# Summing the seven products of a Strassen–Winograd pair in the accumulator banks, with the partial sums copied by ScalarE

## The chip, the cores and the metric

The kernel runs on one core of a Trainium2 chip. The metric is the device time of one execution in microseconds (us); lower is better. Engines are called PE (TensorE), DVE (VectorE), ACT (ScalarE), POOL (GpSimd) and SP (SyncE, here a queue that issues transfers).

## The reference

One layer of an encoder with two gated branches, run on two batches: a long one of 1024 rows and a short one of 512, with shared weights. Cut to what matters here:

```python
h = rms_norm(x, pre_w)
cols = jnp.einsum('bsd,dc->bsc', h, w_in)          # one wide projection
m_qk, m_v, m_o, m_z, m_i, m_f, a_qkv, a_z, gate = jnp.split(cols, ...)
y_m = mlstm_mixer(m_qk, m_v, m_o, m_i, m_f, ...) * silu(m_z)    # branch A, chunks of 128 rows
y_a = dilated_attention(a_qkv, rel_table) * silu(a_z)           # branch B
merged = g[:, :, 0] * (y_m @ w_pm) + g[:, :, 1] * (y_a @ w_pa)  # g = sigmoid(gate)
out = merged @ w_out
return x + rms_norm(out, post_w)
```

Everything is float32. `m_i` and `m_f` are the gates of branch A; their scans (a cumulative sum, a running maximum, exponentials) are the "lanes" below. The change is in the projection `h @ w_in` of the long batch alone.

## The kernel before

**The projection of the long batch.** `h` (1024 rows) and the weights are cut into 2 x 2 blocks, and each block product is made with seven half-size products instead of eight, in Winograd's form: `B11, T2, B21, T3, T1, T4, B22` name the seven combinations of blocks of `h`, which are made once and kept. Each product is float32 by three passes: both operands are split into a rounded high part and a rest (`vhi`, `vlo`; `phla`, `phlb` hold both parts), and `mm3` (L193 to L195) issues high x high, high x rest, rest x high into one bank of the accumulator (PSUM, eight banks, tiles named `d`). With m1 to m7 the seven products, the four output blocks need m1+m2, m1+m6+m7+m5, m1+m6+m7+m4 and m1+m6+m5+m3.

**Value groups** (`value_group`, before 246 us): four groups of columns (values and the gates of branch A), seven products each; a product is 48 matmuls of 128x322 into four banks, 12 to a bank. Group 0 has a path of its own. In groups 1 to 3 the order is B11, B21, T2, T3, T1, T4, B22; ACT copies the four banks of m1 (L555), DVE does the other 28 additions (L564 to L602). `out` splits each finished block into `vz` (ACT L458, DVE L459) and stores it; the buffers `vz`, `vzm` and `co` are few (3, 2, 3), so an ACT copy into `vz` waits until the store of an earlier one has landed. Weights are split ahead by `split` (ACT `vhi` L426, DVE `vlo` L427).

**Pairs** (`unit_pair`, 246 to 975 us): 38 pairs of 128-column units, seven products each, a product is 12 matmuls of 128x512 into one bank. In the order B11, T2, B21, T3, T1, T4, B22; ACT copies m1 (L651) and DVE makes seven additions (L654 to L665). The weights of the next pair are prepared beside it (POOL sums L628 to L646; ACT L609 and DVE L610 split them). What follows a pair on ACT and DVE depends on its kind: 12 "att" pairs, 8 "conv" pairs (`conv_unit`: for each of two halves ACT L676, DVE L678 twice, ACT L679, DVE L680), 8 "zo", 2 "az", 8 gates.

**Lanes** (`lanes`, L837 on) is a generator in four steps, run between the products of value groups 1 and 2. Step 1 transposes the gates on PE (L855), reads the result on ACT (L857, L858), and runs a chain over ACT and DVE (L860 to L879) that ends in `l_tt`; step 2 transposes `l_u` and `l_tt` on PE (L883, L884); step 3 transposes `l_mrow` (L904); step 4 transposes what a second chain made of it (L926, L927). The position of the steps is set by

```python
for g in range(1, 3):
    for j, _ in enumerate(values[g]):
        if j % 3 == 0:
            next(lanes, None)
```

where `j` counts the products of a group (in group 1 the first product has been issued ahead of the loop, so `j = 0` stands behind its second).

Each engine runs its instructions in the order in which they were issued; a scheduler places the copies, splits and additions of ACT and DVE among each other, and PE goes through the products in the order of the code. The stage after 975 us (branches, output projections; `dense`) is not touched.

Of the kernel before, what the change touches and what calls it, by code (L numbers as in the profile page):

```python
# [22 lines left out]
F32 = mybir.dt.float32  # L23
F32R = mybir.dt.float32r
AF = mybir.ActivationFunctionType
# [4 lines left out]
P = 128  # L30
D = 1024
KT = D // P
BLK = 512
# [12 lines left out]
VW = 322  # L46
# [25 lines left out]
class Tokens:  # L72


    def __init__(self, dram, S, x, y, name):
        self.S, self.x, self.y, self.n, self.nblk, self.name = S, x, y, S // P, S // BLK, name
        t = lambda shape, what, dt=F32: dram.tile(shape, dt, name=f"{what}_{name}")
        self.qk = t([16, P, S], "qk")
        self.vs = t([2, S, D], "vs")
        self.G = t([8, P, S], "G")  # L80
        self.aqk = t([2, 24, P, S], "aqk")
        self.av = t([S, 1536], "av")
        self.az = t([4, P, S], "az")
# [20 lines left out]
        return self.bufs[i][dt]  # L104


class Unit:


# [67 lines left out]
class Net:  # L177
# [9 lines left out]
        kw = {} if space is None else {"space": space}  # L187
        return stack.enter_context(self.tc.tile_pool(name=name, bufs=bufs, side=side, reuse_waits="tile", **kw))

    def mm3(self, out, lhs, rhs, start, stop):  # L190
        nc = self.nc
        (lh, ll), (rh, rl) = lhs, rhs
        nc.tensor.matmul(out, lh, rh, start=start, stop=False)  # L193
        nc.tensor.matmul(out, lh, rl, start=False, stop=False)  # L194
        nc.tensor.matmul(out, ll, rh, start=False, stop=stop)  # L195

# [206 lines left out]
    def value_group(self, g, T, H, sb, us, co, ps, late=None, begin=None, u3=None, more=None, turn=None):  # L403
# [17 lines left out]
        def split(x, at=None, parts=1):  # L421
            hi, lo = at or place()
            with self.tc.high_priority():
                for i in range(parts):
                    c = slice(i * N // parts, (i + 1) * N // parts)
                    ends = (nc.scalar.activation(hi[:, c], x[:, c], AF.Copy),  # L426
                            nc.vector.tensor_sub(lo[:, c], x[:, c], hi[:, c].bitcast(F32)))  # L427
# [3 lines left out]
        def product(m, w, turns=(), outer=False):  # L431

            banks = [ps.tile([P, BLK], F32, name="d") for _ in range(4)]
            turns = iter(turns)
            if outer:
                next(turns)
            for i in range(4):
                for j in range(4):
                    t, k = (j, i) if outer else (i, j)
                    ts = slice(t * P, (t + 1) * P)  # L440
                    self.mm3(banks[t][:, :VW], (H[0][m][:, k, ts], H[1][m][:, k, ts]), (w[0][:, k], w[1][:, k]),
                             k == 0, k == 3)
                next(turns, None)
            return banks

# [24 lines left out]
        if g == 0:  # L470
# [77 lines left out]
                add(u3[t], u3[t], m6[t][:, :VW])  # L548
            yield
            co = co()  # L550
        else:
            self.sums(wa, wb, s)
            m1 = product(B11, split(wa[:, 0], first))
            for t in range(4):
                nc.scalar.activation(u2[t], m1[t][:, :VW], AF.Copy)  # L555
            w12 = split(wa[:, 1])
            s2 = split(s[:, 1])
            nc.vector.tensor_sub(s[:, 1], wa[:, 1], s[:, 1])
            yield
            m2 = product(B21, w12)  # L560
            co = co()
            for t in range(4):
                c = tile_("co", 3)
                add(c, u2[t], m2[t][:, :VW])  # L564
                out(t, 0, 0, c)
            yield
            m6 = product(T2, s2)
            for t in range(4):
                add(u2[t], u2[t], m6[t][:, :VW])
            yield  # L570
            m7 = product(T3, split(wb[:, 0]))
            u3 = []
            for t in range(4):
                u3.append(tile_("u3", 4))
                add(u3[t], u2[t], m7[t][:, :VW])
            yield
        if g == 0:
            with self.tc.issue_after(low[2]):
                s1 = split(s[:, 0])
        else:  # L580
            s1 = split(s[:, 0])
        m5 = product(T1, s1)
        if g == 0:
            for t, c in enumerate(held):
                out(t, 0, 0, c)
        for t in range(4):
            add(u2[t], u2[t], m5[t][:, :VW])
            c = tile_("co", 3)
            add(c, u3[t], m5[t][:, :VW])
            out(t, 1, 1, c)  # L590
        yield
        if late is not None:
            store = lambda *x: late.append(x)
        m4 = product(T4, split(wb[:, 1]))
        for t in range(4):
            add(u3[t], u3[t], m4[t][:, :VW])  # L596
            out(t, 0, 1, u3[t])
        yield
        m3 = product(B22, split(s[:, 1]))
        yield  # L600
        for t in range(4):
            add(u2[t], u2[t], m3[t][:, :VW])  # L602
            out(t, 1, 0, u2[t])

    def pair_split(self, x, hl):
        n = x.shape[1]
# [7 lines left out]
    def pair_weights(self, ua, ub, sb):  # L614


        ws = []
        us = [sb.tile([P, BLK], F32, name=f"pu{i}", bufs=4 - i) for i in (2, 3)]
# [10 lines left out]
        self.nc.gpsimd.tensor_sub(s[:, 1], s[:, 0], ws[0][:, 0])  # L629
        s12 = self.pair_split(s, at[1])  # L630
        self.nc.gpsimd.tensor_sub(ws[1][:, 0], ws[0][:, 0], ws[1][:, 0])
        return (*ws, a1, s12, s, bs, us), last

    def unit_pair(self, weights, H, sb, cp, ps):

        nc = self.nc
        wa, wb, (a11, a12), (s1, s2), s, places, (u2, u3) = weights
        split = self.pair_split

        def product(m, w):  # L640
            p = ps.tile([P, BLK], F32, name="d")
            for k in range(4):
                self.mm3(p, (w[0][:, k], w[1][:, k]), (H[0][m][:, k], H[1][m][:, k]), k == 0, k == 3)
            return p

        nc.gpsimd.tensor_sub(s[:, 1], wa[:, 1], s[:, 1])  # L646
        s3, a22 = split(wb, places[0])
        c = [cp.tile([P, 2 + 2 * BLK], F32, name="c") for _ in range(2)]
        q = [[c[j][:, 1 + b * BLK:1 + (b + 1) * BLK] for b in range(2)] for j in range(2)]
        m1 = product(B11, a11)  # L650
        nc.scalar.activation(u2, m1, AF.Copy)  # L651
        m6 = product(T2, s2)
        m2 = product(B21, a12)
        nc.vector.tensor_add(q[0][0], u2, m2)  # L654
        nc.vector.tensor_add(u2, u2, m6)
        m7 = product(T3, s3)
        nc.vector.tensor_add(u3, u2, m7)
        m5 = product(T1, s1)
        nc.vector.tensor_add(q[1][1], u3, m5)
        nc.vector.tensor_add(u2, u2, m5)  # L660
        m4 = product(T4, a22)
        nc.vector.tensor_add(q[1][0], u3, m4)
        s4, = split(s[:, 1:2], places[1])
        m3 = product(B22, s4)
        nc.vector.tensor_add(q[0][1], u2, m3)  # L665
        return c


# [1164 lines left out]
def body(tc, a):  # L1833
# [3 lines left out]
    with ExitStack() as st:  # L1837
# [12 lines left out]
        with ExitStack() as s1:  # L1850
# [4 lines left out]
            with ExitStack() as sv:  # L1855
# [45 lines left out]
                for _ in values[0]:  # L1901
                    pass
                s3.close()
                more, turn = N.pool(sv, "more", 1, "left"), itertools.cycle(range(5))
                values += [N.value_group(g, A, H, vw, us, co, ps, late if g == 3 else None, more=more, turn=turn)
                           for g in range(1, 4)]
                next(values[1])
                with ExitStack() as s4:
                    lanes = N.lanes(A, N.pool(s4, "lane", 1, "right"), lambda: ps.tile([P, BLK], F32, name="d"))
                    for g in range(1, 3):  # L1910
                        for j, _ in enumerate(values[g]):
                            if j % 3 == 0:
                                with tc.issue_after(N.splits[0].ins), tc.issue_after(N.splits[1].ins):
                                    next(lanes, None)
                    for _ in lanes:
                        pass
                    N.bias_tables(N.pool(s4, "tab", 1, "right"), ps, dram)
# [199 lines left out]
```

## Time and profile before

| | us |
|---|---|
| median of 3 runs | 2289.6 (2284.14 to 2295.39) |
| profiled execution, time | 2292.12 |
| profiled execution, span from first to last instruction | 2290.3 |
| PE busy in the span | 2258.5 (99%) |
| DVE busy | 1465.7 (64%) |
| ACT busy | 1102.2 (48%) |
| POOL busy | 628.6 (27%) |
| granted clock of PE, mean | 0.997 |

The profile is of one execution. A row of the timeline begins with the start in us from the first instruction and the length in us (of all the instructions counted at its end); behind it stand the engine, the line, what is written and read, and in brackets how long the engine had been idle and what ended that. A row of the table by windows has the busy time of each engine in a stretch with its number of instructions; matmuls overlap, so a busy PE there need not be PE at its peak, but a PE that waits is seen.

### The profile page before, as it was taken

How to read it: one execution, taken by the hardware profiler on the slowest of the kernel's cores; microseconds unless marked ns; L12 is line 12 of the kernel's file. 1: busy time of each engine (PE TensorE's matmuls, PEld its weight loads, DVE VectorE, ACT ScalarE, POOL GpSimd, SP SyncE). 2: the span in 40 equal slices, each digit the busy share in tenths (PEclk: the TensorE clock that was granted, in tenths of full speed). 3: DMA queues.
4: the chain of work that ended last, by engine and by line, in shares of the span. 5: the costliest groups of instructions: out<-in, count | busy, mean ns of one | idle time of the engine just before them, and what ended most of it. 6: DMA issues, size and time to landing. Idle time of an engine off the chain costs nothing. (4 is left out here: it accounts for less than half of the span.)

```text
span 2290.3 us, 36121 instructions
## 1 busy us (share of the span) xinstructions
PE 2258.5 (99%) x12628; PEld 1975.3 (86%) x12628; DVE 1465.7 (64%) x2851; ACT 1102.2 (48%) x2255; POOL 628.6 (27%) x824
## 2 busy tenths in 40 slices
PE   9999999999999999999999999999999999999998
PEld 8999888888878888879999889988888888888887
DVE  7765577688875564466777756674487744555563
ACT  6332243444443343366667656776544444544422
POOL 2000333333332232136556510001032221421311
PEclk9999999999999999999999999999999999999999
DMA  3552455543222243285674679987687878787673
GB/s 126 161 134 71 173 204 194 195 167 113 101 102 83 83 147 110 91 315 154 219 226 138 199 195 243 249 227 214 181 254 242 254 217 241 201 256 210 216 259 113
DMA packets 251903, 416.71 MB, mean 182 GB/s; under 512 B 24993, under 2 KB 150049, under 8 KB 251722
## 3 DMA queue, kind: packets, MB, share of 16 engines
q1 hardware_dynamic: 248120, 401.82, 56.9%
q10 hardware_dynamic: 3602, 12.59, 1.4%
q8 instruction: 100, 1.64, 0.3%
q14 instruction: 81, 0.66, 0.1%
HBM read 294.34 MB, written 128.37 MB: 185 GB/s over the span
## 5 line engine op out<-in xcount | busy, mean ns | idle before, releaser
L193 PE MATMUL dense<-H,wh 128*128 128x512 f32 x672 | 277.5, 413 | 2.3 <-DVE sw L714 1.9
L195 PE MATMUL dense<-H,wl 128*128 128x512 f32 x672 | 263.8, 393 | 0.0
L194 PE MATMUL dense<-H,wh 128*128 128x512 f32 x672 | 263.0, 391 | 0.0
L195 PE MATMUL d<-Hh,phla 128*128 128x512 f32 x608 | 237.0, 390 | 2.2 <-DVE phla L610 2.2
L193 PE MATMUL d<-Hh,phla 128*128 128x512 f32 x608 | 236.6, 389 | 0.0
L194 PE MATMUL d<-Hl,phla 128*128 128x512 f32 x608 | 236.6, 389 | 0.0
L250 DVE TENSOR_TENSOR wl<-wraw,wh 128x1024 fp32r<-128x1024 f32 (+1 forms) x130 | 163.9, 1262 | 106.7 <-ACT wh L249 105.4
L1475 DVE CUSTOM_DVE_ANT_0 ls<-lg,bias 128x256 f32<-128x256 f32 (+1 forms) x288 | 93.7, 361 | 158.9 <-PE lg L1463 53.9
L249 ACT ACTIVATE wh<-wraw 128x1024 fp32r<-128x1024 f32 (+1 forms) x130 | 137.0, 1054 | 97.1 <-PE dense L194 50.0
L628 POOL TENSOR_TENSOR psum_w<-pw_raw 128x512 f32<-128x512 f32 x38 | 61.4, 1617 | 443.4 <-DVE u L596 216.0
L1479 ACT ACTIVATE ls<-ls,nm 128x256 f32<-128x256 f32 (+1 forms) x288 | 130.0, 453 | 102.9 <-DVE nm L1477 87.8
L195 PE MATMUL d<-Hh,phlb 128*128 128x512 f32 x456 | 177.4, 389 | 0.0
L193 PE MATMUL d<-Hh,phlb 128*128 128x512 f32 x456 | 177.4, 389 | 0.0
L194 PE MATMUL d<-Hl,phlb 128*128 128x512 f32 x456 | 177.4, 389 | 0.0
L195 PEld LDWEIGHTS dense<-H,wl 128*128 128x128 f32 x672 | 126.2, 188 | 28.7
L193 PEld LDWEIGHTS dense<-H,wh 128*128 128x128 f32 x672 | 126.6, 188 | 20.4 <-issue 2.3
L194 PEld LDWEIGHTS dense<-H,wh 128*128 128x128 f32 x672 | 127.0, 189 | 17.5
L194 PE MATMUL d<-vlo,Hh 128*128 128x322 f32 x448 | 139.9, 312 | 1.9 <-DVE vlo L427 1.9
L193 PE MATMUL d<-vhi,Hh 128*128 128x322 f32 x448 | 141.0, 315 | 0.3
L195 PE MATMUL d<-vhi,Hl 128*128 128x322 f32 x448 | 140.3, 313 | 0.4 <-DVE Hl L354 0.2
L195 PEld LDWEIGHTS d<-Hh,phla 128*128 128x128 f32 x608 | 114.1, 188 | 27.3 <-DVE phla L610 3.7
L194 PEld LDWEIGHTS d<-Hl,phla 128*128 128x128 f32 x608 | 114.1, 188 | 23.7
(573 smaller groups left out, 6064.2 us busy)
## 6 DMA issues: line engine op xcount, KB each, us to landing
pw_raw<-w_in SPq DMA_DIRECT2D x76, 512.0 KB
wraw<-w_in SPq DMA_DIRECT2D x76, 512.0 KB
aqk_a<-pwk SPq DMA_DIRECT2D x48, 512.0 KB
aqk_b<-sw SPq DMA_DIRECT2D x48, 256.0 KB
wraw<-w_pm SPq DMA_DIRECT2D x24, 512.0 KB
wraw<-w_out SPq DMA_DIRECT2D x24, 512.0 KB
wraw<-w_v SPq DMA_DIRECT2D x18, 512.0 KB
erep<-erow SPq DMA_DIRECT2D x16, 512.0 KB
```

The costliest lines, as they stand in the source:

```text
L193: nc.tensor.matmul(out, lh, rh, start=start, stop=False)
L194: nc.tensor.matmul(out, lh, rl, start=False, stop=False)
L195: nc.tensor.matmul(out, ll, rh, start=False, stop=stop)
L249: self.splits = (nc.scalar.activation(hi[:, :n], raw[:, :n], AF.Copy), nc.vector.tensor_sub(lo[:, :n], raw[:, :n], hi[:, :n].bitcast(F32)))
L250: nc.vector.tensor_sub(lo[:, :n], raw[:, :n], hi[:, :n].bitcast(F32)))
L628: self.nc.gpsimd.tensor_add(s[:, 0], ws[1][:, 0], ws[1][:, 1])
L1475: nc.vector.tensor_tensor_reduce(out=ls[:, hh], in0=ts["lg"][hh], in1=bt[:, hh], scale=1.0, scalar=NEG, op0=OP.add, op1=OP.max, accum_out= ...
L1479: nc.scalar.activation(ls[:, hh], ls[:, hh], AF.Exp, bias=nm[:, hh:hh + 1], accum_out=ot[:, 128 + hh:129 + hh])
```

## The change

The products are reordered and partial sums are built in the banks. A new class `Banks` hands out the eight banks by hand: `hold` takes one, `done` gives it back. With `onto`, a product goes on adding in a bank that already holds a sum. In a pair the order becomes B11, B21, T2, T1, T3, B22, T4:

```diff
-        m1 = product(B11, a11)
-        nc.scalar.activation(u2, m1, AF.Copy)
-        m6 = product(T2, s2)
-        m2 = product(B21, a12)
-        nc.vector.tensor_add(q[0][0], u2, m2)
-        nc.vector.tensor_add(u2, u2, m6)
-        m7 = product(T3, s3)
-        nc.vector.tensor_add(u3, u2, m7)
-        m5 = product(T1, s1)
-        nc.vector.tensor_add(q[1][1], u3, m5)
-        nc.vector.tensor_add(u2, u2, m5)
-        m4 = product(T4, a22)
-        nc.vector.tensor_add(q[1][0], u3, m4)
-        s4, = split(s[:, 1:2], places[1])
-        m3 = product(B22, s4)
-        nc.vector.tensor_add(q[0][1], u2, m3)
+        sum_ = product(B11, a11)
+        nc.scalar.activation(e1, sum_, AF.Copy)
+        m2 = product(B21, a12)
+        nc.vector.tensor_add(q[0][0], e1, m2)
+        ps.done([m2])
+        product(T2, s2, sum_)
+        nc.scalar.activation(e6, sum_, AF.Copy)
+        m5 = product(T1, s1)
+        nc.scalar.activation(e5, m5, AF.Copy)
+        product(T3, s3, sum_)
+        nc.vector.tensor_add(q[1][1], e5, sum_)
+        s4, = split(s[:, 1:2], places[1])
+        product(B22, s4, m5)
+        nc.vector.tensor_add(q[0][1], e6, m5)
+        ps.done([m5])
+        product(T4, a22, sum_)
+        nc.scalar.activation(q[1][0], sum_, AF.Copy)
+        ps.done([sum_])
```

So a pair has four copies on ACT and three additions on DVE, where it had one and seven. A product that adds onto a bank has to wait until the copy or addition that reads the bank's earlier sum is done: T2 for the copy `e1`, T3 for `e6`, B22 for `e5`, T4 for the addition into `q[1][1]`. The value groups 1 to 3 get the same order and sums, bank by bank (12 additions and 16 copies a group, where there were 28 and 4); group 0 keeps its own. The lanes' steps move too:

```diff
-                            if j % 3 == 0:
+                            if j in ((0, 1, 5), (0, 2, 6))[g - 1]:
```

On PE, step 1 of the lanes stays where it was, in the middle of value group 1. Step 2 stood 144 matmuls (three products) behind it, ahead of the product T4 (`Hh_617`):

```order
L193 MATMUL d<-vhi,Hh_100 128x322
L194 MATMUL d<-vlo,Hh_100 128x322
L195 MATMUL d<-vhi,Hl_107 128x322
L883 MATMUL d<-ident,l_u_1151 1x64
L884 MATMUL d<-ident,l_tt 1x64
L193 MATMUL d<-vhi,Hh_617 128x322
```

It stands 48 matmuls (one product, T2, `Hh_97`) behind it in the changed kernel, ahead of T1 (`Hh_100`):

```order
L211 MATMUL d<-vhi,Hh_97 128x322
L212 MATMUL d<-vlo,Hh_97 128x322
L213 MATMUL d<-vhi,Hl_104 128x322
L918 MATMUL d<-ident,l_u_1151 1x64
L919 MATMUL d<-ident,l_tt 1x64
L211 MATMUL d<-vhi,Hh_100 128x322
```

Two products that stood ahead of the two transposes now stand behind them. Likewise step 3 is now 194 matmuls behind step 2, and step 4 one product (48 matmuls) behind step 3.

On ACT, the chain of the lanes' step 1 ran like this in the kernel before (`l_e`, `l_l` are the lanes' tiles, `vzm` and `vhi` belong to the value group):

```order
L458 ACTIVATE vzm<-co 128x322
L860 ACTIVATE l_e<-l_lf 64x128
L861 ACTIVATE l_e<-l_e 64x128
L863 ACT_TABLE_LOAD
L863 ACTIVATE l_l<-l_u_1151 64x128
L865 ACT_TABLE_LOAD
L865 ACTIVATE l_e<-l_l 64x128
L426 ACTIVATE vhi<-vsum 128x1288
```

In the changed kernel the copies of T2's banks (`u2b<-d`) stand in it:

```order
L476 ACTIVATE vzm<-co 128x322
L592 ACTIVATE u2b<-d 128x322
L895 ACTIVATE l_e<-l_lf 64x128
L592 ACTIVATE u2b<-d 128x322
L896 ACTIVATE l_e<-l_e 64x128
L898 ACT_TABLE_LOAD
L898 ACTIVATE l_l<-l_u_1151 64x128
L592 ACTIVATE u2b<-d 128x322
L900 ACT_TABLE_LOAD
L900 ACTIVATE l_e<-l_l 64x128
L444 ACTIVATE vhi<-vb 128x1288
```

Three copies have come in, and the split `vhi` of the next weights still stands behind the chain.

In a conv pair, ACT ran this from one split of weights to the next in the kernel before:

```order
L609 ACTIVATE phlb<-pw_raw 128x1024
L609 ACTIVATE phlb<-psum_w 128x512
L676 ACTIVATE pwk<-c,cws 128x1024
L651 ACTIVATE pu_4500<-d 128x512
L679 ACTIVATE pwk<-pwk 128x1024
L676 ACTIVATE pwk<-c,cws 128x1024
L609 ACTIVATE phla<-pw_raw 128x1024
L679 ACTIVATE pwk<-pwk 128x1024
L609 ACTIVATE phla<-psum_w 128x1024
```

In the changed kernel (L684, L689, L691, L699 are the copies `e1`, `e6`, `e5` and the one of the last sum; L711 and L714 are the old L676 and L679):

```order
L642 ACTIVATE phlb<-pw_raw 128x1024
L711 ACTIVATE pwk<-c,cws 128x1024
L642 ACTIVATE phlb<-psum_w 128x512
L699 ACTIVATE c<-d 128x512
L684 ACTIVATE pu_4447<-d 128x512
L714 ACTIVATE pwk<-pwk 128x1024
L711 ACTIVATE pwk<-c,cws 128x1024
L642 ACTIVATE phla<-pw_raw 128x1024
L689 ACTIVATE pu_4448<-d 128x512
L714 ACTIVATE pwk<-pwk 128x1024
L642 ACTIVATE phla<-psum_w 128x1024
L691 ACTIVATE pu_4449<-d 128x512
```

The copy `e5`, for which B22 waits, stands last of the pair's work on ACT, behind the second half's tanh (L714) and the split of the next sums.

More of the change, by code (lines that the diff above doesn't have):

```diff
@@ L104, in __call__, with __init__, tile, hold @@
         return self.bufs[i][dt]
+class Banks:
+    def __init__(self, pool):
+        self.free = [pool.tile([P, BLK], F32, name="d") for _ in range(8)]
+    def tile(self, *_, **__):
+        b = self.hold()
+        self.free.append(b)
+        return b
+    def hold(self):
+        return self.free.pop(0)
+    def done(self, banks):
+        self.free.extend(banks)
 class Unit:
@@ L188, in pool, with mm3 @@
         return stack.enter_context(self.tc.tile_pool(name=name, bufs=bufs, side=side, reuse_waits="tile", **kw))
-    def mm3(self, out, lhs, rhs, start, stop):
+    def mm3(self, out, lhs, rhs, start, stop, more=False):
         nc = self.nc
         (lh, ll), (rh, rl) = lhs, rhs
-        nc.tensor.matmul(out, lh, rh, start=start, stop=False)
-        nc.tensor.matmul(out, lh, rl, start=False, stop=False)
-        nc.tensor.matmul(out, ll, rh, start=False, stop=stop)
+        nc.tensor.matmul(out, lh, rh, start=start, stop=False, skip_group_check=more)
+        nc.tensor.matmul(out, lh, rl, start=False, stop=False, skip_group_check=more)
+        nc.tensor.matmul(out, ll, rh, start=False, stop=stop, skip_group_check=more)
     def put(self, key, out, src, of, queue=None):
@@ L429, in split, with product @@
             return hi.rearrange("p (k c) -> p k c", c=VW), lo.rearrange("p (k c) -> p k c", c=VW)
-        def product(m, w, turns=(), outer=False):
-            banks = [ps.tile([P, BLK], F32, name="d") for _ in range(4)]
+        def product(m, w, turns=(), outer=False, onto=None):
+            banks = onto or [ps.hold() if g else ps.tile([P, BLK], F32, name="d") for _ in range(4)]
             turns = iter(turns)
@@ L441, in product @@
                     self.mm3(banks[t][:, :VW], (H[0][m][:, k, ts], H[1][m][:, k, ts]), (w[0][:, k], w[1][:, k]),
-                             k == 0, k == 3)
+                             onto is None and k == 0, k == 3, True)
                 next(turns, None)
@@ L550, in value_group @@
             co = co()
[L551 to L566, printed above, removed]
-            m6 = product(T2, s2)
[L568 to L576, printed above, removed]
@@ L577, in value_group @@
-        if g == 0:
             with self.tc.issue_after(low[2]):
                 s1 = split(s[:, 0])
-        else:
-            s1 = split(s[:, 0])
-        m5 = product(T1, s1)
-        if g == 0:
+            m5 = product(T1, s1)
             for t, c in enumerate(held):
                 out(t, 0, 0, c)
-        for t in range(4):
-            add(u2[t], u2[t], m5[t][:, :VW])
-            c = tile_("co", 3)
-            add(c, u3[t], m5[t][:, :VW])
-            out(t, 1, 1, c)
+            for t in range(4):
+                add(u2[t], u2[t], m5[t][:, :VW])
+                c = tile_("co", 3)
+                add(c, u3[t], m5[t][:, :VW])
+                out(t, 1, 1, c)
@@ new lines, in value_group @@
+            yield
+            m4 = product(T4, split(wb[:, 1]))
+            for t in range(4):
+                add(u3[t], u3[t], m4[t][:, :VW])
+                out(t, 0, 1, u3[t])
+            yield
+            m3 = product(B22, split(s[:, 1]))
+            yield
+            for t in range(4):
+                add(u2[t], u2[t], m3[t][:, :VW])
+                out(t, 1, 0, u2[t])
+            return
+        self.sums(wa, wb, s)
+        copy = lambda to, of: nc.scalar.activation(to, of[:, :VW], AF.Copy)
@@ new lines, in value_group @@
+        sum_ = product(B11, split(wa[:, 0], first))
+        for t in range(4):
+            copy(u2[t], sum_[t])
+        w12 = split(wa[:, 1])
+        s2 = split(s[:, 1])
+        nc.vector.tensor_sub(s[:, 1], wa[:, 1], s[:, 1])
+        yield
+        m2 = product(B21, w12)
+        co = co()
+        for t in range(4):
+            c = tile_("co", 3)
+            add(c, u2[t], m2[t][:, :VW])
+            out(t, 0, 0, c)
+        ps.done(m2)
+        yield
+        product(T2, s2, onto=sum_)
@@ L591, in value_group @@
+        for t in range(4):
+            copy(u2[t], sum_[t])
+        yield
+        m5 = product(T1, split(s[:, 0]))
+        e5 = [tile_("u3", 4) for _ in range(4)]
+        for t in range(4):
+            copy(e5[t], m5[t])
         yield
@@ L593, in value_group @@
             store = lambda *x: late.append(x)
-        m4 = product(T4, split(wb[:, 1]))
+        product(T3, split(wb[:, 0]), onto=sum_)
         for t in range(4):
-            add(u3[t], u3[t], m4[t][:, :VW])
-            out(t, 0, 1, u3[t])
+            add(e5[t], e5[t], sum_[t][:, :VW])
+            out(t, 1, 1, e5[t])
         yield
-        m3 = product(B22, split(s[:, 1]))
+        product(B22, split(s[:, 1]), onto=m5)
+        for t in range(4):
+            add(u2[t], u2[t], m5[t][:, :VW])
+            out(t, 1, 0, u2[t])
+        ps.done(m5)
+        yield
+        product(T4, split(wb[:, 1]), onto=sum_)
         yield
         for t in range(4):
-            add(u2[t], u2[t], m3[t][:, :VW])
-            out(t, 1, 0, u2[t])
+            c = tile_("co", 3)
+            copy(c, sum_[t])
+            out(t, 0, 1, c)
+        ps.done(sum_)
     def pair_split(self, x, hl):
@@ L617, in pair_weights @@
         ws = []
-        us = [sb.tile([P, BLK], F32, name=f"pu{i}", bufs=4 - i) for i in (2, 3)]
+        us = [sb.tile([P, BLK], F32, name=f"pu{i}", bufs=1) for i in range(3)]
         bs = [sb.tile([P, 2, 2, BLK], F32R, name="phlb", bufs=2) for _ in range(2)]
@@ L636, in unit_pair, with product @@
         nc = self.nc
-        wa, wb, (a11, a12), (s1, s2), s, places, (u2, u3) = weights
+        wa, wb, (a11, a12), (s1, s2), s, places, (e1, e6, e5) = weights
         split = self.pair_split
-        def product(m, w):
-            p = ps.tile([P, BLK], F32, name="d")
+        def product(m, w, onto=None):
+            p = ps.hold() if onto is None else onto
             for k in range(4):
-                self.mm3(p, (w[0][:, k], w[1][:, k]), (H[0][m][:, k], H[1][m][:, k]), k == 0, k == 3)
+                self.mm3(p, (w[0][:, k], w[1][:, k]), (H[0][m][:, k], H[1][m][:, k]), onto is None and k == 0, k == 3, True)
             return p
@@ L1903, in body @@
                 s3.close()
+                ps = Banks(ps)
                 more, turn = N.pool(sv, "more", 1, "left"), itertools.cycle(range(5))
```

1 line of the change is left out of this document (removed).

## The prediction

> **What bounds the kernel now.** I read the busy shares first, then the busy time by windows over the stages that the change touches, then the waits of PE, and last the timelines of PE, ACT and DVE at the places where the order moves.
>
> ```profile
> PE 2258.5 (99%) x12628; PEld 1975.3 (86%) x12628; DVE 1465.7 (64%) x2851; ACT 1102.2 (48%) x2255; POOL 628.6 (27%) x824
> ...
> 104.00:125.00 21.00, 19.13 (x125) 18.37 (x124) 16.82 (x34) 11.68 (x20) 0.00 (x0) 1.00 0.77 169
> 125.00:185.00 60.00, 60.00 (x399) 59.20 (x399) 39.65 (x80) 17.96 (x30) 0.00 (x0) 1.00 0.51 138
> 246.00:611.00 365.00, 365.00 (x1613) 302.13 (x1612) 277.44 (x274) 148.22 (x148) 131.39 (x109) 1.00 0.45 165
> 611.00:700.00 89.00, 86.81 (x381) 70.84 (x380) 69.76 (x72) 37.31 (x40) 30.42 (x22) 1.00 0.29 103
> 700.00:973.00 273.00, 273.00 (x1206) 226.07 (x1205) 148.02 (x174) 101.25 (x112) 71.14 (x59) 1.00 0.29 103
> ```
>
> After the window stand its length and the busy time of PE, its weight loads, DVE, ACT and POOL. PE is busy without a hole in three of the five windows and lacks 1.9 and 2.2 us in the other two. So PE's own matmuls are the bound of both stages, and the change issues as many matmuls of the same shapes as before. From the same rows come the two pitches: 60.00 / 399 = 0.150 us for a 128x322 matmul, so 7.2 us for a product of 48 in a value group; 365 / 1613 = 0.226 us for a 128x512 one, so 2.72 us for a product of 12 in a pair and 19.04 us for a pair. PE's waits on what the change touches are these (total, times, longest):
>
> ```profile
> PE d L195 <- DVE phla L610: 2.2, 3, 1.0
> PE d L194 <- DVE vlo L427: 1.9, 3, 0.9
> ```
>
> Their sum, 4.1 us, is all that a lighter DVE could give in these stages: 0.2% of the time.
>
> **The work removed and added.**
>
> ```profile
> L654 DVE TENSOR_TENSOR c<-pu,d 128x512 f32<-128x512 f32 x38 | 26.1, 687 | 104.3 <-PE d L195 100.2 <-issue 4.0
> L651 ACT ACTIVATE pu<-d 128x512 f32<-128x512 f32 x38 | 22.8, 600 | 7.9 <-PE d L195 7.9
> L564 DVE TENSOR_TENSOR co<-u2b,d 128x322 f32<-128x322 f32 x8 | 3.9, 484 | 2.0 <-PE d L195 2.0
> L555 ACT ACTIVATE u2b<-d 128x322 f32<-128x322 f32 x5 | 2.2, 434 | 4.4 <-PE d L195 4.4
> ```
>
> DVE loses 38 x 4 additions of 0.687 us and 3 x 16 of 0.484: 104.4 + 23.2 = 127.6 us. ACT gains 38 x 3 copies of 0.600 and 3 x 12 of 0.434: 68.4 + 15.6 = 84 us. Neither counts by itself: both engines work beside PE, as the windows show (DVE 277 of 365, ACT 148 of 365), and DVE's waits on PE ahead of L654 (100.2 us) say who is ahead. What counts is which product now waits for whom. Splits and additions that were late go with DVE's load: I book the 2.2 us of phla whole, and of vlo's 1.9 the two later ones, 1.7; the first stands ahead of the moved order and may stay. Bounds for both together: -4.1 and 0.
>
> **The lanes' step 2 (the largest term).** Step 1 is on PE at 104.48; step 2 came at 128.99:
>
> ```profile
> 104.48 0.27 PE L855 MATMUL d<-ident,gall 128*128 128x128 f32 x1
> ...
> 128.99 0.21 PE L883 MATMUL d<-ident,l_u 64*1 64x64 f32 x1
> ```
>
> Between lie three products and 2.4 us of stalls and transposes. The chain on ACT, and its end on DVE:
>
> ```profile
> 106.71 0.47 ACT L458 ACTIVATE vz<-co 128x322 fp32r<-128x322 f32 x1 [0.37 <-DMA vs_a<-vz]
> 110.12 0.47 ACT L458 ACTIVATE vz<-co 128x322 fp32r<-128x322 f32 x1 [2.93 <-DMA vs_a<-vz]
> 110.50 1.26 ACT L426 ACTIVATE vhi<-vb 128x1288 fp32r<-128x1288 f32 x1
> 111.67 0.34 ACT L857 ACTIVATE l_li<-d,gb 32x128 f32<-32x128 f32 x1
> ...
> 114.56 1.28 ACT L863 ACT_TABLE_LOAD   x1
> ...
> 116.19 1.28 ACT L865 ACT_TABLE_LOAD   x1
> 117.48 0.31 ACT L865 ACTIVATE l_e<-l_l 64x128 f32<-64x128 f32 x1
> ```
>
> ```profile
> 118.67 0.48 DVE L569 TENSOR_TENSOR u2b<-u2b,d 128x322 f32<-128x322 f32 x1
> ...
> 120.17 1.47 DVE L427 TENSOR_TENSOR vlo<-vsum,vhi 128x1288 fp32r<-128x1288 f32 x1
> 121.60 0.11 DVE L897 MEMSET l_mrow<- 1x64 f32 x1
> 121.64 0.08 DVE L879 TENSOR_TENSOR l_tt<-l_u,l_l 64x1 f32<-64x1 f32 x1
> ```
>
> The reader is to see that ACT begins the chain 7.2 us after PE's transpose, since it is held at 110.12 by a store that has to land, and that `l_tt` is ready at 121.7, while PE asks only at 129: 7.3 us of slack. In the changed kernel PE asks one product after step 1, at 104.48 + 7.2 plus the short stall there, about 112.3. On ACT everything up to 111.67 is as before, then three copies of 0.43 come into the chain (+1.3, L865 ends at 119.1); on DVE the addition (0.4) and the split (1.47) leave it, so that the last five instructions take about 2.1 us. `l_tt` is ready near 121.2, and PE sees it at 121.3: it stands for **9.0 us**, with T1 and all later products behind it. No other work of PE covers that. Bounds: without the copies in the chain and the store landing 2.9 us earlier, 4.8; with the chain's old DVE part (1.9 more), 10.9.
>
> **What a long stall does to PE's pace.** No wait of before is so long. Two rows bound it: after the first idle time of the kernel the transposes run at half pace,
>
> ```profile
> 3.38 3.75 PE L1882 MATMUL d<-Hh,u 1*128 1x512 f32 x4 [3.38 <-DMA Hh<-prew]
> 7.05 5.28 PE L349 MATMUL d<-u2b,x 128*128 128x128 f32 x23
> ...
> 12.12 1.26 PE L349 MATMUL d<-u2b,x 128*128 128x128 f32 x9
> ```
>
> 23 of them from 7.05 to 12.12, 0.22 us each, the next 9 about 0.12 each ((1.26 - 0.27) / 8). From 3.38 to 12.12 is 8.7 us at half pace, a loss of 4.4. After the longest idle time in mid-kernel there is none: matmuls follow each other at 0.22 to 0.31 at once.
>
> ```profile
> 1009.21 0.47 PE L193 MATMUL dense<-H,wh 128*128 128x512 f32 x1 [1.90 <-DVE sw L714]
> 1009.52 0.39 PE L194 MATMUL dense<-H,wh 128*128 128x512 f32 x1
> 1009.74 0.40 PE L195 MATMUL dense<-H,wl 128*128 128x512 f32 x1
> ```
>
> Bounds 0 and 4.4; a stall of 9 us is nearer to the first case in length, but PE has long been in full use here, so I take the middle, +2.2. [...]
>
> **Steps 3 and 4.** Step 3 comes 194 matmuls after step 2: 29 us, no wait. Step 4 comes one product (7.2 us) after step 3. By the rows of its chain (DVE copy of `mb`, one split of 1.5 us ahead of the rest, two exponentials and their halves on ACT, 2.3 us) it is ready about 6 us after step 3. I take 0, bounds 0 and 2.
>
> **The copies in the pairs.** T2 waits for e1, T3 for e6, B22 for e5, T4 for an addition; each has one product (2.72 us) of cover. In att, zo, az and gate pairs ACT reaches each copy in time (e1 about 1 us before T2 is due in the fullest kind). In the conv pairs e5 stands last in a chain:
>
> ```profile
> L609 ACT ACTIVATE phla<-psum_w 128x1024 fp32r<-128x1024 f32 x37 | 39.2, 1058 | 116.7 <-PE d L195 116.7
> L676 ACT ACTIVATE pwk<-c,cws 128x1024 f32<-128x1024 f32 x16 | 19.8, 1237 | 7.7 <-DVE c L665 7.6
> L678 DVE SCALAR_TENSOR_TENSOR pwk<-c,cws,pwk 128x1024 f32<-128x1024 f32 x32 | 52.8, 1650 | 6.3 <-ACT pwk L676 6.0
> L679 ACT ACTIVATE pwk<-pwk 128x1024 f32<-128x1024 f32 x16 | 17.0, 1063 | 46.2 <-DVE pwk L678 46.2
> L680 DVE SCALAR_TENSOR_TENSOR pwk<-pwk 128x1024 f32<-128x1024 f32 x16 | 21.4, 1336 | 9.1 <-ACT pwk L679 9.1
> L610 DVE TENSOR_TENSOR phla<-pw_raw,phla 128x1024 fp32r<-128x1024 f32 x37 | 55.1, 1488 | 1.4 <-ACT phla L609 1.4
> ```
>
> Count from the end of B22 of one pair. B11 of the next ends at 5.44, e1 on ACT at 6.3; then L679 (to 7.4), L680 on DVE (to 8.8), the first addition (0.69, 9.5), L678 (11.1), the rest of phla (12.6), L678 (14.3), L679 (15.3), phla<-psum_w (16.4), e5 (0.60, 17.0). B22 is due at 16.32: a stall of 0.7 to 0.9. With the shortest durations (POOL still, L678 1.28, phla 1.21) e5 ends at 15.8 and nothing stalls; where POOL's sums run beside DVE, L678 took 2.31:
>
> ```profile
> 621.01 2.16 POOL L629 TENSOR_TENSOR psum_w<-psum_w,pw_raw 128x512 f32<-128x512 f32 x1
> ...
> 621.94 2.31 DVE L678 SCALAR_TENSOR_TENSOR pwk<-c,cws,pwk 128x1024 f32<-128x1024 f32 x1
> ```
>
> and the stall is 1.6. I take 0.8, eight times: **+6.4**, bounds 0 and 12.8.
>
> **The sum.** 9.0 - 1.7 + 2.2 + 6.4 - 2.2 = +13.7 us on the profiled execution of 2292.1: 2305.8. That execution lay 2.5 us above the median of 2289.6, so the forecast is **2303**, 0.6% slower, just past the 0.5% (11.4 us) that a measurement of this kernel tells from no change.
>
> **Rivals.**
> - *The lanes are early* (not slower). The place is ACT's wait at 110.12. If the store lands when the one before it did, the chain starts 2.9 us sooner and the copies run behind it: a stall of 4.8, no loss of pace, e5 in time thanks to a DVE with 4 x 0.69 us less per pair. 2292.1 + 4.8 - 3.9 = 2293, so 2290.5. It decides where all new waits together stay under 11.4 + 3.9 = 15.3 us. For it: stores share the queue with others, and their times move. Against: 7.3 us of slack against 16.7 us taken away.
> - *The conv pairs wait fully.* 9.0 + 2.2 + 12.8 - 3.9 = +20.1: 2309.7. For it: L678's mean of 1.65 says that POOL meets it often. Against: DVE has less to do, so its part may fall beside POOL's pauses.
> - *The sums cost nothing and DVE's waits go.* -3.9: 2285.7. It needs the lanes' chain 9 us earlier; nothing in the rows gives that.
>
> **Chances.** Forecast (2297 to 2309) 0.50, the lanes early 0.25, conv full 0.15, no new wait 0.05, something unseen 0.05. Two thirds of the first case lie above 2301: 0.33; with conv full and a share of the unseen, slower 0.50. Same: 0.17 + 0.25 + 0.04 = 0.46. Faster 0.04, since 4.1 us is the most that goes. The range 2289 to 2313 leaves out part of the last two and the upper third of conv full.
>
> **What would show it.** On PE a wait at L918/L919 for DVE's L908 or L914 of about 9 us near 112, and matmuls at 0.3 us behind it; PE waits on ACT L691 at B22 in conv pairs; no waits on L643 and L445 of before's size; DVE about 128 us less busy, ACT 84 more; from 975 us on the same length. Wrong if step 2 does not wait, or if e1 or e6 wait in att pairs, which would add up over 12 pairs.

## The result, and the profile after

The changed kernel takes 2309.2 us (median of 6 runs, 2306.2 to 2313.4) against 2293.5 of the kernel before (6 runs, 2284.1 to 2298.2): the ratio is 1.0074, with a 95% interval of 1.0053 to 1.0095. It is slower, as forecast; the forecast of 2303 was 0.6% above the median it started from (2289.6, three runs), and the result is 0.7% above the median of the six runs. The profiled execution took 2307.7 us, 15.6 more than that of before.

The busy shares, and the table by windows (window, length, busy time of PE, weight loads, DVE, ACT, POOL, granted clock, then transfers), of the changed kernel:

```profile
PE 2260.4 (98%) x12628; PEld 1973.4 (86%) x12628; DVE 1345.1 (58%) x2651; ACT 1178.7 (51%) x2405; POOL 626.2 (27%) x824
...
104.00:125.00 21.00, 11.96 (x70) 11.15 (x69) 13.50 (x33) 11.92 (x24) 0.00 (x0) 0.84 0.78 168
125.00:185.00 60.00, 60.00 (x399) 59.47 (x399) 28.29 (x46) 24.16 (x46) 0.00 (x0) 1.00 0.41 106
246.00:611.00 365.00, 360.44 (x1601) 297.61 (x1600) 216.95 (x195) 178.31 (x205) 127.33 (x108) 1.00 0.47 170
611.00:700.00 89.00, 88.38 (x388) 72.20 (x387) 57.15 (x52) 43.66 (x52) 28.17 (x24) 1.00 0.28 98
700.00:973.00 273.00, 273.00 (x1206) 225.83 (x1205) 119.57 (x120) 126.23 (x159) 79.14 (x62) 1.00 0.29 103
```

DVE is 120.6 us less busy and ACT 76.5 more, and PE, which had a hole of 1.9 us in the first window, has one of 9.0 there, at a granted clock of 0.84. The waits of PE in the changed stages (total, times, longest):

```profile
PE d L918 <- DVE l_u L908: 7.2, 1, 7.2
...
PE d L211 <- ACT pu L691: 2.5, 8, 0.8
PE d L211 <- ACT pu L684: 2.2, 1, 2.2
...
PE d L890 <- DVE co L604: 1.1, 1, 1.1
...
PE d L919 <- DVE l_tt L914: 0.7, 1, 0.7
...
PE d L213 <- DVE phla L643: 0.5, 1, 0.5
```

The waits for `vlo` and nearly all of those for `phla` are gone. In their place stand the lanes' two transposes, the copy e5 (L691) in eight pairs, and one that the prediction did not have: the copy e1 (L684), once, 2.2 us. Where the time stands at the end of the two stages is read from the copy e1, which follows PE's first product of each pair; the row has the start of the first and of the last of 38, first before, then after:

```profile
L651 ACT ACTIVATE pu<-d x38: 573/598/646, 249.3 to 957.0; 128x512 f32<-128x512 f32 x38
```

```profile
L684 ACT ACTIVATE pu<-d x38: 577/598/792, 258.1 to 970.2; 128x512 f32<-128x512 f32 x38
```

The last pair comes 13.2 us later (970.2 - 957.0), so 13.2 of the 15.6 us are lost in the stages that the change touches and 2.4 behind them. All kernels below are compared at this mark, each by one profiled execution. Ahead of the changed stages these executions already differ by up to 0.9 us (a matmul that starts at 68.35 before starts at 68.81 in the second experiment below and at 67.90 in the seventh), so a difference of marks under 1 us says nothing by itself.

**The lanes.** PE's transposes, ACT's chain and the chain's end on DVE in the changed kernel:

```profile
105.61 0.30 PE L890 MATMUL d<-ident,gall 128*128 128x128 f32 x1 [1.12 <-DVE co L604]
120.37 0.26 PE L918 MATMUL d<-ident,l_u 64*1 64x64 f32 x1 [7.22 <-DVE l_u L908]
121.32 0.26 PE L919 MATMUL d<-ident,l_tt 64*1 64x64 f32 x1 [0.69 <-DVE l_tt L914]
```

```profile
110.15 0.47 ACT L476 ACTIVATE vz<-co 128x322 fp32r<-128x322 f32 x1 [2.50 <-DMA vs_a<-vz]
...
111.70 0.34 ACT L892 ACTIVATE l_li<-d,gb 32x128 f32<-32x128 f32 x1
...
114.73 0.42 ACT L592 ACTIVATE u2b<-d 128x322 f32<-128x322 f32 x1
...
118.60 0.31 ACT L900 ACTIVATE l_e<-l_l 64x128 f32<-64x128 f32 x1
```

```profile
121.11 0.15 DVE L914 TENSOR_TENSOR l_tt<-l_u,l_l 64x1 f32<-64x1 f32 x1
```

ACT is held by the same landing store until 110.15 and begins the chain at 111.70 (111.67 before); `l_tt` is there at 121.3, where it was reckoned at 121.2. PE stands from 113.1 on (120.37 less 7.22). And behind the wait it runs at half pace:

```profile
112.90:121.50 8.60, 0.69 (x4) 0.15 (x2) 4.18 (x13) 7.36 (x15) 0.00 (x0) 0.77 1.00 233
121.50:124.40 2.90, 2.90 (x12) 2.89 (x12) 2.33 (x10) 0.00 (x0) 0.00 (x0) 0.50 0.12 31
124.40:128.00 3.60, 3.60 (x26) 3.60 (x26) 0.00 (x0) 0.88 (x2) 0.00 (x0) 1.00 0.00 0
```

The clock column reads 0.50 from 121.5 to 124.4, with 12 matmuls in 2.9 us (0.24 each), and 1.00 behind it, with 26 in 3.6 (0.14). At full pace (0.15) the 12 would have taken 1.8, so the half clock cost about 1.1 us of work; the rest of it fell into the wait.

**The second pair.** The new wait for e1 has its cause in the queue of stores. SP's queue, ACT and PE:

```profile
260.64 10.75 SPq L1964 DMA_DIRECT2D av_a<-co  x1
```

```profile
275.37 0.58 ACT L699 ACTIVATE c<-d 128x512 f32<-128x512 f32 x1
280.31 1.15 ACT L748 ACTIVATE pwk<-c 128x960 fp32r<-128x960 f32 x2 [4.35 <-issue]
281.36 0.58 ACT L684 ACTIVATE pu<-d 128x512 f32<-128x512 f32 x1
```

```profile
281.99 0.50 PE L211 MATMUL d<-Hh,phla 128*128 128x512 f32 x1 [2.18 <-ACT pu L684]
```

The last value group's fourth sum is now copied into `co` and stored last of all; the store's row on the queue begins at 260.6 and runs for 10.7 us. The pairs' work buffers (`pwk`) take over that memory, so L748 sits still for 4.35 us although its input is there at 275.95, and e1 stands behind it. The store's row ends at 271.4, but the trace has the last update of the semaphore that its landing counts up at 280.23, and L748 starts at 280.31. The fifth experiment moves that sum elsewhere.

### The profile page after: what moved, and what is told of

Read it like the earlier page. It is cut to its first block, busy times and chain, and to the rows that moved or that the text cites. A ratio compares the mean times of both kernels' runs of the same rounds, so it can differ in the third digit from the quotient of the medians.

```text
span 2305.9 us, 35972 instructions
## 1 busy us (share of the span) xinstructions
PE 2260.4 (98%) x12628; PEld 1973.4 (86%) x12628; DVE 1345.1 (58%) x2651; ACT 1178.7 (51%) x2405; POOL 626.2 (27%) x824
## 5 line engine op out<-in xcount | busy, mean ns | idle before, releaser
L661 POOL TENSOR_TENSOR psum_w<-pw_raw 128x512 f32<-128x512 f32 x38 | 51.2, 1347 | 522.8 <-DMA pw_raw<-w_in 472.6
L211 PEld LDWEIGHTS d<-Hh,phla 128*128 128x128 f32 x608 | 114.1, 188 | 26.2 <-ACT pu L684 2.6
L213 PEld LDWEIGHTS d<-Hh,phla 128*128 128x128 f32 x608 | 114.1, 188 | 24.4 <-DVE phla L643 0.9
```

Of the source, the lines that this page charges most:

```text
L211: nc.tensor.matmul(out, lh, rh, start=start, stop=False, skip_group_check=more)
L213: nc.tensor.matmul(out, ll, rh, start=False, stop=stop, skip_group_check=more)
```

## Experiments

The theory: the loss is the lanes' step 2, asked for one product after step 1, with the half clock behind it; then e5 in the conv pairs and the late store. The rival: the sums themselves, by their copies on ACT, make the stages slower wherever the lanes stand.

**1. Lanes apart.** The steps cannot simply go back, since from T1 until the sums of B22 are read all eight banks hold sums; they go behind B22 and into group 2.

```diff
-                            if j in ((0, 1, 5), (0, 2, 6))[g - 1]:
+                            if j in ((0, 4), (0, 2, 6))[g - 1]:
```

> The changed kernel with the lanes' step 2 four products behind step 1 instead of one, and steps 3 and 4 each two products behind the one before. Theory (the lanes' early step 2 holds PE): no wait of PE at the two transposes, no half clock near 120 us, PE through the value groups about 9.5 us sooner than in the changed kernel; time 2300 against 2293.5 before, ratio 1.002 to 1.004. Rival (the new copies and sums cost it, the lanes are harmless): the ratio stays at 1.007.

The ratio is 1.0045 (1.0030 to 1.0061), over the expected 1.002 to 1.004; the last e1 starts at 964.7, 5.5 us sooner than in the changed kernel and not 9.5. No transpose waits any more. But with PE no longer standing at step 2, the lanes' chain on ACT delays the split of the weights for T3 (the seventh experiment moves the chain, and this wait goes). The half clock near 120 us, which was expected to go, is there too, behind that wait, and the second pair's wait now has one behind it as well:

```profile
121.54 0.46 PE L212 MATMUL d<-vlo,Hh 128*128 128x322 f32 x1 [1.80 <-DVE vlo L445]
...
275.31 0.76 PE L211 MATMUL d<-Hh,phla 128*128 128x512 f32 x1 [2.36 <-ACT pu L684]
```

```profile
121.80:125.20 3.40, 3.40 (x14) 3.40 (x14) 1.65 (x3) 0.00 (x0) 0.00 (x0) 0.50 0.00 1
275.30:278.80 3.50, 3.50 (x8) 2.78 (x9) 2.38 (x4) 1.15 (x2) 1.45 (x1) 0.51 0.15 59
```

The second row has eight 128x512 matmuls in 3.5 us, 0.44 each where 0.226 is full pace: another 1.7 us.

**2. The lanes' move alone**, in the kernel before:

```diff
-                            if j % 3 == 0:
+                            if j in ((0, 1, 5), (0, 2, 6))[g - 1]:
```

> The kernel before, with nothing changed but the positions of the lanes' steps, as in the changed kernel. Theory: step 2 is asked for at about 112.3 us and l_tt is ready at 121.7 at the earliest, so PE waits 8 to 10 us there, then runs some us at half clock: ratio 1.004 to 1.005, about +10 us. Rival (the step is harmless by itself, the copies in the lanes' chain hold it up): under 2 us, ratio 1.000.

```profile
118.73 0.26 PE L883 MATMUL d<-ident,l_u 64*1 64x64 f32 x1 [6.27 <-DVE l_u L873]
120.96 0.26 PE L884 MATMUL d<-ident,l_tt 64*1 64x64 f32 x1 [1.97 <-DVE l_tt L879]
```

```profile
112.20:121.00 8.80, 0.56 (x4) 0.12 (x2) 6.42 (x17) 5.83 (x10) 0.00 (x0) 0.64 1.02 232
121.00:125.00 4.00, 4.00 (x15) 3.88 (x16) 1.46 (x10) 0.00 (x0) 0.00 (x0) 0.50 0.06 18
```

Ratio 1.0044 (1.0033 to 1.0056); waits of 8.2 us, half clock behind them, the last e1 at 965.2, 8.2 later than before. With no copy in the chain the step costs the same. This is the largest part of the loss, and neither the copies nor the additions cause it. The sums have their part in it all the same: the banks that they hold are why the step lost its place.

**3. The value groups alone**, lanes apart as in the first, pairs as before (the pairs' code of before in the kernel of the first experiment).

> New sums in the value groups only, the lanes' steps apart as in the first of these runs, the pairs as before. Theory: the waits of vlo (1.9 us) go and nothing else comes but up to 2 us at the second pair, where ACT waits for the landing of the last late store: ratio 0.999 to 1.001. Rival (16 copies on ACT instead of 4 hold PE in the groups): PE 3 us or more later at 246 us, ratio 1.002 or more.

Ratio 1.0013 (1.0004 to 1.0023), the last e1 at 957.1, 0.1 from before. The sums in the groups cost PE nothing on balance. The waits for `vlo` were expected to go, and one of 1.8 us stays, with 16 additions a group less on DVE. The upper end of the interval lies above what was expected.

**4. The pairs alone**, lanes and value groups as before.

> New order and sums in the pairs only, value groups and lanes as before. Theory: the wait for the copy e5 in the eight conv pairs (3 to 4 us in sum) comes, the waits of phla (2.2) go, no wait at the second pair, since the late stores are those of before: +1 to +2 us, ratio 1.000 to 1.001. Rival (the pairs' copies carry the loss): +8 us or more, ratio 1.004.

```profile
PE d L211 <- ACT pu L676: 2.0, 8, 0.3
```

Ratio 1.0005 (0.9994 to 1.0016), the last e1 at 957.5, 0.5 later: the eight waits for e5 (L676 in this kernel, 2.0 us) weigh as much as the waits for `phla` that go, or a little more. No wait at the second pair, since no `co` is stored late. The losses do not add up by themselves: 8.2 + 0.1 + 0.5 is 8.8 of the 13.2; more than half of the rest is the wait at the second pair, which needs both halves: the late store of `co` from the new groups, and a product (T2) that waits for e1, from the new pairs. (In the third experiment ACT's copy waits there too, 2.11 us, and no product with it.)

**5. The late sum elsewhere.** The first experiment's kernel, the fourth sum of group 3 in the free buffers of group 2:

```diff
-            c = tile_("co", 3)
+            c = tile_("u2", 4) if g == 3 else tile_("co", 3)
             copy(c, sum_[t])
```

> The first of these kernels (lanes apart, ratio 1.0045), with group 3's last sum copied into the buffers of the group before instead of co. Theory: ACT's wait at the second pair is for the landing of that sum's late store, whose memory the pairs' work buffers take over; without it PE's wait there (2.5 us) and the half clock behind it (1.7) go: about -4 us, ratio 1.0025 to 1.003. Rival (the pairs' store queue is late by itself): the wait stays and the ratio stays at 1.0045.

The wait at the second pair is gone, so the late store of that sum is its cause (the last of these stores is issued at 246.0 here, at 253.6 in the first experiment). But all four copies now run on ACT ahead of the first pair's split, and B11, the next product on PE, waits for that, again with half clock behind:

```profile
245.57 0.44 ACT L592 ACTIVATE u<-d 128x322 f32<-128x322 f32 x1 [1.38 <-PE d L213]
245.90 1.05 ACT L642 ACTIVATE phla<-pw_raw 128x1024 fp32r<-128x1024 f32 x1
```

```profile
247.00 0.50 PE L211 MATMUL d<-Hh,phla 128*128 128x512 f32 x1 [1.47 <-ACT phla L642]
...
248.26 0.50 PE L213 MATMUL d<-Hh,phla 128*128 128x512 f32 x1 [0.53 <-DVE phla L643]
```

```profile
248.80:252.20 3.40, 3.40 (x9) 2.63 (x8) 1.68 (x2) 0.04 (x1) 2.78 (x2) 0.50 0.16 56
```

Ratio 1.0052 (1.0034 to 1.0070) where 1.0025 to 1.003 was expected: the wait moved. The last e1 is at 961.3, 3.4 sooner than in the first experiment, but the time does not show it. (In the changed kernel only three of the copies stood there, since the fourth had to wait for a buffer.)

**6. e5 early.** The same, and

```diff
-        nc.scalar.activation(e5, m5, AF.Copy)
+        with self.tc.high_priority():
+            nc.scalar.activation(e5, m5, AF.Copy)
```

> The same, and in the pairs the copy e5 is put ahead of the split of the next sums on ACT. Theory: e5 comes 1 us sooner in the conv pairs, all eight waits of PE for it go (2.3 us in the waits, 3 in PE's pace) and nothing else waits: ratio 1.001 to 1.0015. Rival (the split that is put back becomes late in its turn): as many waits on phla, the same time as the run beside it.

PE's listed waits for e5 fall from 1.9 us in eight to 0.4 in two, so the place of that copy on ACT is their cause, for the most part (shorter ones are left, see the tenth experiment). Ratio 1.0029 (1.0016 to 1.0043): better than the run beside it by less than the intervals tell apart, and not the 1.001 expected, for the first pair's wait of 1.5 us and that for `vlo` (2.0) are still there. The last e1 starts at 961.0 (961.3 without this edit), so these two executions do not show the gain; this one has its half clock at 123 us, that one at 249.

**7. Lanes later.** The same, and the chain moved away from T3:

```diff
-                            if j in ((0, 4), (0, 2, 6))[g - 1]:
+                            if j in ((4,), (0, 2, 6))[g - 1]:
```

> The same, and the lanes' step 1 behind the sixth product of group 1, steps 2 to 4 behind the first, third and last of group 2. Theory: the lanes' chain no longer stands ahead of the split of T3's weights on ACT, so that the wait for vlo near 119 us (2.0 us, half clock 1.3) goes and no transpose waits, since two products (14.4 us) lie between steps 1 and 2: 0.998 to 1.000, the kernel before less its own waits for vlo and phla at best. Rival (the chain is as late there, held by stores): a wait of 2 us or more at step 2.

No wait for `vlo`, 0.6 us at step 2; the last e1 at 955.8, 1.2 us ahead of the kernel before. The ratio is still 1.0019 (1.0005 to 1.0033), a miss: the first pair's wait stays, and the timed runs (2288.2 to 2302.5, median 2295.4) lie mostly above the profiled one (2289.4), by more than that explains.

**8. Lanes later in the kernel before**, with nothing else changed: `if j in ((4,), (0, 2, 6))[g - 1]:` for `if j % 3 == 0:`.

> The kernel before with the lanes at those later places and nothing else. Theory: its wait for vlo near 120 us (1.1 us) goes, its waits for phla stay: ratio 0.999 to 1.000. If the run beside it is no faster than this one, the new sums are worth nothing even without their waits.

Ratio 0.9994 (0.9981 to 1.0007), the last e1 at 954.7, 2.3 us ahead of the kernel before without any new sum. Most of it stands at the first pair already (first e1 at 247.3 against 249.3): of the 1.9 us of waits for `vlo` 0.5 are left, of the 2.2 for `phla` 1.9.

**9. The last copies on DVE.** The kernel of the seventh, and

```diff
-            copy(c, sum_[t])
+            if g == 3:
+                nc.vector.tensor_copy(c, sum_[t][:, :VW])
+            else:
+                copy(c, sum_[t])
```

> The kernel with the later lanes (ratio 1.0019), and group 3's last four copies on DVE instead of ACT. Theory: on ACT these copies stand ahead of the first pair's split, and B11 behind T4 waits 1.5 us for it, then runs at half clock: -2.5 us at the first pair, nothing else moves; PE 3 to 4 us ahead of the kernel before at 975 us, ratio 1.000 to 1.001. Rival (the first pair waits for its weights' load): the wait stays.

```profile
L687 ACT ACTIVATE pu<-d x38: 600/601/747, 246.3 to 954.8; 128x512 f32<-128x512 f32 x38
```

```profile
PE d L211 <- ACT pu L695: 1.2, 2, 0.9
```

The first pair's split is in time; the last e1 at 954.8, 2.2 ahead of the kernel before, not 3 to 4, since the first pair now waits for e5. Ratio 1.0005 (0.9996 to 1.0015): with nearly all of its new waits taken away the whole change is even.

**10. The pairs, e5 early and lanes later**, the value groups' sums as before.

> New order and sums in the pairs only, with the copy e5 put early, the value groups' sums as before, the lanes at the later places. Theory: no new wait is left (no late store of a fourth sum, no e5, no transposes), and the waits of vlo and phla of the kernel before are gone: PE 3 to 4 us ahead at 975 us, ratio 0.998 to 0.999, the best of all. Rival (what was gained there is given back at the start of the branches, where PE waits for H whenever it comes): 1.000.

```profile
L669 ACT ACTIVATE pu<-d x38: 600/601/842, 246.4 to 953.7; 128x512 f32<-128x512 f32 x38
```

The list of PE's waits has none for `vlo`, `phla` or a copy in the two stages, and the last e1 starts at 953.7, 3.3 ahead of the kernel before. Ratio 0.9990 (0.9980 to 1.0000). It has the lowest ratio of all, but it is not told apart from the eighth, nor surely from no change.

The 3.3 us are not the work of the sums. From the first pair's e1 to the last one's the tenth kernel takes 707.3 us (953.7 - 246.4), the eighth, without any new sum, 707.4 (954.7 - 247.3), the kernel before 707.7. In the pairs the new sums save the waits for `phla` and spend as much on e5, which is still late in eight pairs, by too little for the list of PE's waits. The rows are PE's weight loads that wait for e5 (L677; total, times), and B22's first matmul in one conv pair, 0.46 us behind the one before it where 0.226 is the pace:

```profile
  PEld d L211: 3.2, 8
```

```profile
581.87 0.39 PE L213 MATMUL d<-Hh,phlb 128*128 128x512 f32 x1
582.33 0.50 PE L211 MATMUL d<-Hh,phlb 128*128 128x512 f32 x1
```

The rival is half right. At the start of the branches PE waits 2.07 us for `H`, where it waited 1.09, and the half clock follows (0.51 from 976.1 to 979.5). At the first long wait behind it the tenth kernel is ahead again (that matmul starts at 1006.27, before at 1009.21), and yet its profiled execution ends 1.2 us behind that of the kernel before (2293.31 against 2292.12). What it was ahead is lost in stages that the change does not touch.

## Why the prediction was right

- *The bound.* PE's matmuls; DVE's 121 us less (128 forecast) and ACT's 77 more (84 forecast) are seen in the time only through waits of PE. The best kernel, the tenth, is 3.3 us ahead at the last pair, under the 4.1 named as the most that could go, and 2.3 of that came in the eighth without any new sum.
- *The lanes.* Forecast 9.0 us, measured 7.2 + 0.7 = 7.9. The chain ended where it was reckoned (121.3 against 121.2); PE asked 0.8 us later than reckoned (113.1 against 112.3), for the most part because step 1 came 1.1 us later (105.61 against 104.48), behind a wait for DVE's addition L604 that the prediction did not have. (Between the two steps of the kernel before lie three products and 2.9 us, not 2.4; the sum does not use it.) The second experiment shows the step alone to cost 8.2. The rival "the lanes are early" is ruled out: the store landed when it did before (110.15).
- *The half clock.* Forecast +2.2, measured 1.1. The kernel start, the upper bound, was a poor neighbour: work ran there up to 12.12 us, 8.7 us from PE's first matmul on, at half pace by the prediction's reading (the 23 transposes at 0.22 us each, the next nine at about 0.12), against 2.9 us here. The lower bound was too simple: one wait of 1.9 us in mid-kernel had no half clock behind it (1.00 from 1009.2 to 1012.6), but the same profile has a half clock of 10.3 us elsewhere, where no listed wait near it is over 1.12 us:

```profile
1889.60:1899.90 10.30, 9.71 (x32) 8.12 (x33) 3.68 (x8) 4.13 (x8) 2.27 (x3) 0.50 0.98 302
```

- *The waits that go.* The 2.2 of `phla` in the conv pairs went, as the fourth experiment shows for the pairs alone, and 0.5 at the first pair is new. For `vlo` 1.7 was forecast and the whole 1.9 went, but that was luck: the forecast laid it to DVE's lighter load, and with the same lighter load and the lanes apart 1.8 to 2.0 us are back (first, third, fifth and sixth experiments), while later lanes take them away with the old sums too, but for 0.5 (eighth). In the changed kernel PE stood some 8 us at step 2, which gave the splits time.
- *e5 in the conv pairs.* The term that was mis-sized: 6.4 forecast, 2.5 us of listed waits measured; by the starts of PE's matmuls the eight pairs lose 4.8 (about 0.5 each, 1.1 in the first). The place, the number (eight) and the cause were right, as the sixth experiment shows. The chain was too long because whole durations were added, while these rows overlap by about 0.1 us each:

```profile
592.16 2.31 DVE L643 TENSOR_TENSOR phla<-pw_raw,phla 128x1024 fp32r<-128x1024 f32 x1
594.39 1.27 DVE L713 SCALAR_TENSOR_TENSOR pwk<-c,cws,pwk 128x1024 f32<-128x1024 f32 x1
```

```profile
597.61 0.57 ACT L691 ACTIVATE pu<-d 128x512 f32<-128x512 f32 x1
```

  Here e5 ends at 598.18, 0.4 us late. From the end of e1 (587.78) nine steps lead to it, whose durations add up to 10.9 us and which take 10.4. POOL's sums (587.62 to 593.39) met the split (2.31 us, where the next one, with POOL still, took 1.22) and one L713 (1.72 us; the other took 1.27), not both.
- *What was missed.* "In att pairs ACT reaches each copy in time" counted ACT's own work and not the memory it writes: the second pair's wait (2.2 us) and 0.5 at the first, together about 3.2 with restarts. A wait for e1 in an att pair was one of the prediction's own signs of being wrong; it came in one pair of twelve. These 3.2 us, and the wait at step 1, made up for the oversized terms (e5, the lanes, the half clock). So the sum was nearer than its parts, by luck: 13.7 forecast for the profiled execution, 13.2 at the last pair, 15.6 at the end. The median of 2309.2 lies 6 us above the 2303, still inside the range of 2289 to 2313; 3.9 us of that are the base, whose median rose from 2289.6 to 2293.5 with three more runs.
- *Open.* The 2.4 us behind the last pair. About 1.0 of them is there when the branches start, where PE waits for the last pair's results (first before, then after; 991.21 - 977.00 is 14.2):

```profile
977.00 1.31 PE L273 MATMUL d<-ident,xs 128*128 128x128 f32 x8 [1.09 <-DVE H L280]
```

```profile
987.21 2.40 PE L291 MATMUL d<-ident,xs 128*128 128x128 f32 x20 [0.25 <-ACT c L699]
991.21 1.31 PE L291 MATMUL d<-ident,xs 128*128 128x128 f32 x8 [1.60 <-DVE H L298]
```

  The rest is open. The stage there is the same code, and among the profiled executions above its length differs from that of before by -1.5 us to +5.7 (span less the mark); nothing was tried that would tell why.

## What to carry to other kernels

Sums kept in the accumulator spared an engine that had time (DVE, 120.6 us less busy) and put waits on the one that had none (PE, 2.5 us of listed waits for e5 and 2.2 for e1): each bank that is added to must have been read, so ask of every such read what stands ahead of it on its engine, and which store its buffer waits for. Steps that share banks with such sums lose their places, and a step moved one product behind its source has that product for its cover, which is to be compared with the source's whole chain (here 7.2 us against 15.7, from step 1 at 105.61 to `l_tt` at 121.3). When a wait is mended, look at the next product in line: here it moved from the second pair to the first.

## What the runs showed of the hardware

PE's clock was granted at half after waits of about 2 us, and not after each of them. Behind 1.47 + 0.53 us at the first pair it was 0.50 for 3.4 us in the fifth experiment; behind the same two waits in the sixth (249.68 and 250.94) it stayed at 1.00, and in the seventh (245.62 and 246.88) the matmuls behind them follow each other at 0.23 us. The row is of the sixth:

```profile
250.90:254.30 3.40, 3.36 (x15) 2.77 (x16) 2.25 (x2) 1.21 (x2) 2.20 (x2) 1.00 0.15 55
```

Behind the 1.80 us for `vlo` it was 0.50 in the first experiment, behind 1.83 at the same place (121.62) in the third it was 1.00. It was 0.51 behind 2.36 us (first), but 1.00 behind the 2.18 us at 281.99 in the changed kernel. The lengths that the rows give lie near 3.4 us and near twice and three times that. The short blocks are 3.4 us (a mean of 0.51 over 3.5 us is (1 - 0.51) x 3.5 / 0.5 = 3.4 too). The longer ones are estimates from the means, if the clock was either 1.00 or 0.50: in the changed kernel a mean of 0.77 over 8.6 us is (1 - 0.77) x 8.6 / 0.5 = 4.0 us at half, and 2.9 follow: 6.9 (the column reads 0.50 throughout from 117.6 to 124.3). In the second experiment, with 8.2 us of waits, a mean of 0.64 over 8.8 us is (1 - 0.64) x 8.8 / 0.5 = 6.3 us at half, and 4.0 follow: 10.3, as long as the block in the kernel before (1889.60 to 1899.90). So a wait of about 2 us cost 2 us or 3.7 (with half of 3.4 behind it); no run was made to show what decides it.
